# Two more places for experts' weights, and the block for tokens over capacity at the fifth quad with its loads on GpSimd

## The chip, the cores and the metric

The kernel runs on one core of one Trainium2 chip. The metric is the device time of one execution in microseconds; each kernel's time is the median of several runs. The engines are TensorE (PE in the profile; its weight loads are PEld), VectorE (DVE), ScalarE (ACT), GpSimd (POOL) and SyncE (SP), which issues nearly all transfers. Sixteen DMA engines move the data between HBM and the on-chip memory, where every tile lies over 128 partitions; a place of 8 KB per partition holds 1 MB.

## The reference

One layer over 256 tokens of width 1024, in float32: a projection to nine parts, a gated linear recurrence (hgrn2) and an attention with a bias by distance (moba, one block here) beside each other, a gated sum and an output projection, a residual with layer norm, a hierarchical mixture of experts, and a second residual with layer norm. The last part is what this change touches:

```
proj = h @ w_in[l] + b_in[l]                       # 1024 x 5632
y_a = hgrn2_mixer(...) @ w_proj_a[l]
y_b = moba_mixer(mb_q, mb_k, mb_v, rel_bias) @ w_proj_b[l]
mixed = (sigmoid(gate_a) * y_a + sigmoid(gate_b) * y_b) @ w_out[l]
x = layer_norm(DN_ALPHA * h + mixed, ...)
# hier_moe: best of 4 groups, best 2 of its 8 experts, 32 experts in all
gate, up = split(xb @ w_gate_up[e], 2)             # 1024 x (2 x 512) for each expert
y = (silu(gate) * up) @ w_down[e]                  # 512 x 1024 for each expert
x = layer_norm(DN_ALPHA * x + sum of the weighted y, ...)
```

Every expert is computed, so all weights are read once: 4 MB of `w_gate_up` and 2 MB of `w_down` for each of the 32 experts, 192 MB in all, beside some 30 MB for the projections.

## The kernel before

**The front.** The projections take their weights through four places `w_t` of 1 MB (`W_PL`), filled by `w_load` (line 108) in the order of use. Each tile is cut into four chunks of 512 columns, and ScalarE and VectorE split each chunk into a high and a low part (`split_next`, lines 280 and 281), since every product is made of three matmuls of such parts. When the fourth chunk of a tile has been split, the next `w_t` is loaded into its place. The work of hgrn2, moba and the router is written as generators that give a few instructions between the chunks (`beside`).

**The experts.** The experts go in eight quads of four (`NQ`). A quad has 24 tiles of 1 MB (`NEXP`): 16 of `w_gate_up`, each with 128 rows of two experts, and 8 of `w_down`. Each expert has room for 32 tokens (`CAP`), so a quad's tokens fill 128 columns; `gather` picks them, `by_expert` (line 1140) multiplies each expert's tokens by its weights into its own 32 partitions, `act_T` makes the activation, `y_out` and `combine` (line 1060) add the weighted result to `acc`.

**The places of the tiles `e_t`.** `E_PL` lists the places for these tiles in the order in which they come free. Four are never used for anything else, 19 to 22; the others are those of the front, once it is done with them. Tile i takes the i-th of the list (two tiles, `E_SPL` and `E_PART`, have halves elsewhere), and after the list has run out the same places go round, without the one of `acc` (`N_ACC`). `e_load(n)` issues the next n loads (line 168), at spots written out by hand: five after the third projection, two at the end of hgrn2, four at the end of moba, and so on until all places are filled, `E_NEXT` being the first tile that goes round. After that the loads stand in SP's queue in the order of the tiles, each waiting for its place; SP takes its instructions in order. Each load waits also for the load eight before it, since eight semaphores are used in turn.

```
E_NEXT = 23
E_PL = (19, 20, 21, 22, XS, H3, H4, M1, M2, M3, M4, XHI, XLO, OH, M5, 2, G1, 3, H2, 0, 1, G2)
```

**The block for tokens over capacity** (`overflow`, from line 1096). If an expert has more than 32 tokens, a loop over the experts gathers, computes and adds the further ones, with its own loads of the expert's weights in pieces of 256 KB. All engines read the highest count from memory and branch (line 1102). No expert has more than 32 tokens with these inputs, so the block is jumped over. It stands before the third quad's first matmul, behind the whole `combine` of the second; elsewhere half of a combine stands behind the second tile pair of the next quad.

Of the kernel before, what the change touches and what calls it, by code (L numbers as in the profile page):

```python
# [20 lines left out]
P = 128  # L21
# [23 lines left out]
N_ACC = 15  # L45
E_SPL = 8
E_PART = 10
E_NEXT = 23
N_WARM = (6, 1, 1, 5, 0, 14, 4)

W_PL = (0, 1, 2, 3)
XHI, XLO, XS = 4, 5, 6
H1, H2, H3, H4 = 7, 8, 9, 10
M1, M2, M3, M4, M5 = 11, 12, 13, 14, 15
OH, G1, G2 = 16, 17, 18
E_PL = (19, 20, 21, 22, XS, H3, H4, M1, M2, M3, M4, XHI, XLO, OH, M5, 2, G1, 3, H2, 0, 1, G2)


@with_exitstack
def kernel(ctx: ExitStack, tc: tile.TileContext, x, w_in, b_in, rows_in, relb, w_proj_a, w_proj_b,  # L60
                             w_out, w_router, b_router, w_gate_up, w_down, out):
    nc = tc.nc
# [8 lines left out]
    def place(i, name):  # L71

        t = big.tile([P, 2048], F32, tag=f"s{i}", name=name)
        return t[:, 0:1024], t[:, 1024:2048], t

    def part(i, name, dt=F32):
        return big.tile([P, 1024], dt, tag=f"m{i}", name=name)
# [39 lines left out]
    def e_place(i):  # L117

        i -= (i > E_SPL) + (i > E_PART)
        n = len(E_PL) - 1  # L120
        return E_PL[i] if i < n else (E_PL[:N_ACC] + E_PL[N_ACC + 1:])[(i - n) % n]

# [7 lines left out]
    def e_halves(i, halves, ns=(0, 1)):  # L130

        ts = e_tiles.setdefault(i, [None] * 2)
        for n in ns:
            nc.sync.dma_start(halves[n], e_source(i)[:, n])
            ts[n] = halves[n]

    def e_get(i):
        q, r = divmod(i, NEXP)
        if i == E_SPL:
            e_halves(i, [part(n, "e_half") for n in (1, 2)])  # L140
            return
        if i == E_PART:
            p = place(E_PL[-1], "e_t")
            e_halves(i, (part(3, "e_half"), p[0]))
            e_halves(E_NEXT, (p[1],), (0,))
            return
        t = place(e_place(i), "e_t")
        if i == E_NEXT:
            e_halves(i, (None, t[0]), (1,))
        elif q == NQ - 1 and 16 <= r < 20:  # L150

            t = t[2].rearrange("p (e c) -> p e c", e=4)
            r0 = (r - 16) * P
            nc.sync.dma_start(t, w_down[0, 4 * q:4 * q + 4, r0:r0 + P, 0:512].rearrange("e p c -> p e c"))
            e_tiles[i] = [t[:, e, :] for e in range(4)]
        elif q == NQ - 1 and r >= 20:

            nk, w = (2, 256) if r < 22 else (4, 128)
            c0, k0 = (512, 2 * (r - 20)) if r < 22 else (768 + 128 * (r - 22), 0)
            t = t[2].rearrange("p (k e c) -> p k e c", k=nk, e=4)  # L160
            for k in range(nk):
                r0 = (k0 + k) * P
                nc.sync.dma_start(t[:, k], w_down[0, 4 * q:4 * q + 4, r0:r0 + P, c0:c0 + w].rearrange(  # L163
                    "e p c -> p e c"))
            e_tiles[i] = [[t[:, k, e, :] for e in range(4)] for k in range(nk)]
        else:
            t = t[2].rearrange("p (e c) -> p e c", e=2)
            nc.sync.dma_start(t, e_source(i))  # L168
            e_tiles[i] = [t[:, e, :] for e in range(2)]
# [3 lines left out]
    def e_load(n=1):  # L173
        for _ in range(n):
            while e_next[0] in (E_SPL, E_PART):
                e_next[0] += 1
            e_get(e_next[0])
            e_next[0] += 1
# [86 lines left out]
    def places(ap, base):  # L265
        nc.gpsimd.iota(ap, pattern=[[1, ap.shape[1]]], base=base, channel_multiplier=0,
                       allow_small_or_imprecise_dtypes=True)
# [164 lines left out]
    q, scr, _ = place(H1, "h1")  # L432
# [22 lines left out]
    def rows_plus(dst, ps, row):  # L455
        for t in range(NT):
            nc.vector.tensor_tensor(dst[:, t, :], ps[:, t, :], row, op=ALU.add)
            yield
# [114 lines left out]
    queue.append(hg)  # L573
    ps = prod_N(KD, xh, xl)
    after.append(rows_plus(v, ps, bi))
    e_load(5)


    mqk = place(M1, "mqk")
# [387 lines left out]
    e_get(E_SPL)  # L967
    assert e_next[0] == E_NEXT and len(splits) == 4 * len(w_srcs)
    h_T(1, 4, 2)
# [108 lines left out]
    def late():  # L1078

        acc.extend(place(E_PL[N_ACC], "acc")[0:2])  # L1080
        for j in range(2):
# [15 lines left out]
    def overflow():  # L1097

        cmx = nc.values_load(cnt[0:1, 32:33], min_val=0, max_val=S)
        tl = work(1)  # L1100
        iov = o12.rearrange("p t a b -> p (t a b)")
        with tc.If(cmx > CAP):
            with tc.For_i(0, NE) as e:
                ce = nc.values_load(cnt[0:1, bass.ds(e, 1)], min_val=0, max_val=S)
                for g in range(2):
                    with tc.If(ce > CAP + g * P):
                        places(iov, CAP + 1 + g * P)
                        nc.vector.tensor_copy(pe[:, :, 0:1], posm[:, :, bass.ds(e, 1)])
                        nc.vector.tensor_copy(pe[:, :, 1:2], wsel[:, :, bass.ds(e, 1)])
                        xg, wT = tl["xg"], wT_of(tl["wT"])  # L1110
                        for _ in gather(lambda t: pe[:, t, 0:1], iov, tl):
                            pass
                        weigh(lambda t: pe[:, t, 1:2], P, tl)
                        gu = big2("gu")
                        for k in range(KD):
                            for j in range(2):
                                w = y_tile()[:, j * 512:(j + 1) * 512]
                                nc.sync.dma_start(w, w_gate_up[0, bass.ds(e, 1), k * P:(k + 1) * P,
                                                               j * 512:(j + 1) * 512].rearrange("e p c -> p (e c)"))
                                nc.tensor.matmul(gu[:, j, :], xg[:, k, :], w, start=(k == 0), stop=(k == KD - 1))  # L1120
                        act_T(gu)
                        py = big2("py")
                        xw = xg.rearrange("p k c -> p (k c)")
                        for k in range(4):
                            for j in range(2):
                                w = xw[:, j * 512:(j + 1) * 512]
                                nc.sync.dma_start(w, w_down[0, bass.ds(e, 1), k * P:(k + 1) * P,
                                                            j * 512:(j + 1) * 512].rearrange("e p c -> p (e c)"))
                                nc.tensor.matmul(py[:, j, :], hT_of(k), w, start=(k == 0), stop=(k == 3))
                        y_out(py)  # L1130
                        combine(wT)

            places(iota1, 1)
# [12 lines left out]
    for q in range(NQ):  # L1146
        tl = work(q)
        n0 = q * NEXP
        if q == 2:
            combine(wT_of(q - 1))  # L1150
            pending = False
            overflow()
        gu = big2("gu")
        for k in range(KD):
            if q == 0 and k == 0:
                next(feed)
                with tc.issue_after(xg_put[0].ins):
                    token_weights()
            elif q == 0 and k == 2:
                with tc.issue_after(ins):  # L1160
                    run(feed)
            for j in range(2):
                ins = by_expert(gu[:, j, :], tl["xg"][:, k, :], e_rows(n0 + 2 * k, j), k == 0, k == KD - 1,
                                pin=q == 0 and j == 0)
            if k == 1 and pending:
                combine(wT_of(q - 1))
                pending = False
            if k == 4 and q + 1 < NQ:
                with tc.issue_after(ins):
                    run(places_of(q + 1, work(q + 1)))  # L1170
                if q:
                    weigh_quad(q + 1, work(q + 1))
            if k == 5 and q == NQ - 1:
                lg2, lb2, _ = place(e_place(NQ * NEXP), "ln2")
                for r, dst in ((16, lg2), (24, lb2)):
                    for a in range(2):
                        nc.scalar.activation(dst[:, a * 512:(a + 1) * 512], spread(r + 4 * a), AF.Copy)
        act_T(gu)
        if q == 0:
            late()  # L1180
            weigh_quad(0, tl)
            weigh_quad(1, work(1))
        py = big2("py")
        if q < NQ - 1:
            for k in range(4):
                for j in range(2):
                    by_expert(py[:, j, :], hT_of(k), e_rows(n0 + 16 + 2 * k, j), k == 0, k == 3)
            y_out(py)
            pending = True
        else:  # L1190
            for k in range(4):
                by_expert(py[:, 0, :], hT_of(k), e_tile(n0 + 16 + k), k == 0, k == 3)
# [112 lines left out]
```

## Time and profile before

| | |
|---|---|
| median of 3 runs | 679.61 us (679.32 to 683.38) |
| the profiled execution | 678.75 us, span 677.1 us |
| TensorE busy | 552.7 us (82%), granted clock 0.966 of full |
| VectorE, ScalarE, GpSimd busy | 229.5, 161.8, 9.3 us |
| moved by DMA | 238.48 MB, 352 GB/s over the span |

The span goes from the first to the last instruction of one profiled execution. The page cuts it into 40 slices of 16.93 us, and gives for each the share of time that an engine was busy, the granted TensorE clock and what the DMA engines moved. Other views used below: windows (busy time of each engine, clock and GB/s in stretches of one's choice), the timeline of one engine in a stretch, the waits of one queue and what ended them, one line's or tile's instructions, and the chain of work that ended last.

### The profile page before, as it was taken

The page shows a single profiled execution, that of the slowest core. Times are in us where ns is not written, and L with a number is a line of the kernel's source. Part 1 is how long each engine was busy: PE and PEld are TensorE (multiplying, and loading weights), DVE is VectorE, ACT ScalarE, POOL GpSimd, SP SyncE. Part 2 cuts the span into 40 slices and gives each one's busy share as a digit, 9 for nine tenths or more (in the row PEclk, how much of TensorE's full clock was granted, in tenths as well). Part 3 has the DMA queues.
Part 4 walks back from the last instruction along what each step waited for, and adds up shares of the span by engine and source line. Part 5 has one row for each costly group of instructions (what it writes and reads, how often), then busy time and mean ns, then how long its engine had stood idle before and what let it go on. Part 6 is the DMA issues. An engine that isn't in the chain of part 4 may idle for free.

```text
span 677.1 us, 9744 instructions
## 1 busy us (share of the span) xinstructions
PE 552.7 (82%) x4018; PEld 313.0 (46%) x4019; DVE 229.5 (34%) x531; ACT 161.8 (24%) x321; POOL 9.3 (1%) x32
## 2 busy tenths in 40 slices
PE   8999999999998989876667767676766678678575
PEld 8989899999988453322211311131121113113123
DVE  3698768865676324120202101010201010010026
ACT  4653568955552200100100100010001001001010
POOL 1000000000000000000000000000000000000000
PEclk9999999999999969998999979998999998799989
DMA  8998366686996899989999999999999999999994
GB/s 305 368 358 262 126 249 208 229 293 204 342 383 239 325 408 409 408 315 410 410 408 410 409 409 409 410 409 409 409 410 409 410 408 410 409 409 409 404 344 132
DMA packets 78832, 238.48 MB, mean 352 GB/s; under 512 B 5182, under 2 KB 12991, under 8 KB 78783
## 3 DMA queue, kind: packets, MB, share of 16 engines
q1 hardware_dynamic: 78767, 237.80, 91.7%
q8 instruction: 33, 0.54, 0.3%
q14 instruction: 16, 0.13, 0.1%
q10 hardware_dynamic: 16, 0.01, 0.0%
HBM read 236.74 MB, written 1.06 MB: 351 GB/s over the span
## 4 chain that ended last, share of the span: by engine, by line
DMA 43%; PE 8%; SPq 2%; DVE 1%; ACT 1%; issue 0%; DVEq 0%; ACTq 0%
DMA e_t<-in_w_gate_up_dram 29%; DMA e_t<-in_w_down_dram 14%; PE gu L1140 4%; PE py L1140 2%; SPq L168 1%; PE pc L1060 1%; PE pr L1070 1%; PE pw L1204 1%; SPq L163 0%; ACT yb L1052 0%; DVE acc L1250 0%; DVE acc L1248 0%; DVE smv L807 0%; DVE yb L1043 0%; DVE yb L1044 0%
## 5 line engine op out<-in xcount | busy, mean ns | idle before, releaser
L1140 PE MATMUL gu<-e_t,xg 128*32 128x512 f32 x1012 | 168.4, 615 | 61.9 <-DMA e_t<-in_w_gate_up_dram 60.0
L1140 PEld LDWEIGHTS gu<-e_t,xg 128*32 128x32 f32 x1012 | 35.1, 110 | 176.4 <-DMA e_t<-in_w_gate_up_dram 114.4
L1140 PE MATMUL py<-e_t,hw 128*32 128x512 f32 x480 | 80.3, 680 | 28.1 <-DMA e_t<-in_w_down_dram 23.3
L281 DVE TENSOR_TENSOR w_spl<-w_t,w_spl 128x512 fp32r<-128x512 f32 x120 | 82.2, 689 | 45.3 <-ACT w_spl L280 44.7
L280 ACT ACTIVATE w_spl<-w_t 128x512 fp32r<-128x512 f32 x120 | 75.2, 631 | 72.7 <-PE psT L324 41.2
L324 PE MATMUL psT<-xT_hi,w_spl 128*128 128x256 f32 x576 | 86.7, 288 | 0.7 <-ACT w_spl L280 0.6
L324 PEld LDWEIGHTS psT<-xT_hi,w_spl 128*128 128x128 f32 x576 | 76.3, 193 | 3.6 <-ACT w_spl L280 2.0
L917 DVE TENSOR_SCALAR xg<-px,cols 128x128 f32<-128x128 f32 x32 | 12.6, 408 | 137.1 <-ACT xg L920 127.4
L1140 PEld LDWEIGHTS py<-e_t,hw 128*32 128x32 f32 x480 | 17.2, 121 | 84.5 <-DMA e_t<-in_w_down_dram 46.5
L920 ACT ACTIVATE xg<-px,cols 128x128 f32<-128x128 f32 x32 | 13.9, 455 | 176.2 <-PE px L896 170.9
L324 PE MATMUL psT<-xT_lo,w_spl 128*128 128x256 f32 x288 | 46.6, 285 | 0.0
L1053 DVE COPY yb<-py 128x512 f32<-128x512 f32 x7 | 4.8, 691 | 105.4 <-ACT yb L1052 105.4
L324 PEld LDWEIGHTS psT<-xT_lo,w_spl 128*128 128x128 f32 x288 | 40.1, 193 | 0.0
L1043 DVE TENSOR_TENSOR yb<-gu,yb 128x512 f32<-128x512 f32 x8 | 5.5, 691 | 98.8 <-ACT yb L1042 98.8
L1060 PE MATMUL pc<-yb,hw 128*128 128x512 f32 (+2 forms) x72 | 31.8, 568 | 4.9 <-ACT yb L1052 4.2
L896 PEld LDWEIGHTS px<-oh,hx 128*128 128x128 f32 x256 | 29.3, 192 | 6.7 <-issue 6.7
L1061 DVE TENSOR_TENSOR acc<-acc,pc 128x512 f32<-128x512 f32 (+2 forms) x36 | 22.5, 628 | 28.6 <-PE pc L1060 28.5
L896 PE MATMUL px<-oh,hx 128*128 128x128 f32 x256 | 31.0, 279 | 0.0
L1052 ACT ACTIVATE yb<-py 128x512 f32<-128x512 f32 x7 | 4.2, 597 | 92.1 <-PE py L1140 92.1
L1042 ACT ACTIVATE yb<-gu 128x512 f32<-128x512 f32 x8 | 4.8, 597 | 85.0 <-PE gu L1140 85.0
L1060 PEld LDWEIGHTS pc<-yb,hw 128*128 128x128 f32 x72 | 12.0, 189 | 24.7 <-ACT yb L1052 9.7
L331 PE MATMUL psN<-w_spl,mix 128*128 128x512 f32 (+1 forms) x105 | 23.3, 376 | 0.1
(235 smaller groups left out, 466.6 us busy)
## 6 DMA issues: line engine op xcount, KB each, us to landing
e_t<-in_w_gate_up_dram SPq DMA_DIRECT2D x126, 1024.0 KB, 18.6
e_t<-in_w_down_dram SPq DMA_DIRECT2D x59, 1024.0 KB, 18.5
w_t<-in_w_in_dram SPq DMA_DIRECT2D x20, 1024.0 KB, 6.2
w_t<-in_w_out_dram SPq DMA_DIRECT2D x4, 1024.0 KB, 5.9
e_t<-in_w_down_dram SPq DMA_DIRECT2D x6, 512.0 KB, 11.3
w_t<-in_w_proj_a_dram SPq DMA_DIRECT2D x2, 1024.0 KB
w_t<-in_w_proj_b_dram SPq DMA_DIRECT2D x2, 1024.0 KB, 5.0
e_t<-in_w_down_dram SPq DMA_DIRECT2D x8, 256.0 KB, 4.9
```

The costliest lines, as they stand in the source:

```text
L168: nc.sync.dma_start(t, e_source(i))
L280: ins = [nc.scalar.activation(hi, w, AF.Copy), nc.vector.tensor_tensor(lo, w, hi.bitcast(F32), op=ALU.subtract)]
L281: nc.vector.tensor_tensor(lo, w, hi.bitcast(F32), op=ALU.subtract)]
L324: nc.tensor.matmul(ps[:, c, :], a[:, c * P:(c + 1) * P], b[k], start=(k == 0 and n == 0 and c % 2 == 0), stop=(k == nk - 1 and n == 2 and ...
L331: nc.tensor.matmul(ps, a[k][:, tsl], b, start=(k == 0 and n == 0), stop=(k == nk - 1 and n == 2), skip_group_check=skip)
L896: nc.tensor.matmul(dst, hx[:, t, k * P:(k + 1) * P], oh[:, t, :], start=(k == g[0] and t == 0), stop=(k == g[-1] and t == 1), skip_group_c ...
L917: xg_put[:] = [nc.vector.tensor_scalar(xg[:, k, :], pk, g1_cols[:, k:k + 1], b1_cols[:, k:k + 1], op0=ALU.mult, op1=ALU.add)]
L920: nc.scalar.activation(xg[:, k, :], pk, AF.Identity, bias=b1_cols[:, k:k + 1], scale=g1_cols[:, k:k + 1])
L1060: nc.tensor.matmul(pc, wT[:, t * P:(t + 1) * P], y_tile()[:, sl], start=True, stop=True)
L1061: nc.vector.tensor_tensor(acc[t][:, sl], acc[t][:, sl], pc, op=ALU.add)
L1070: nc.tensor.matmul(pr[:, k * P:(k + 1) * P], ident[0:32, r + k:r + k + 1].to_broadcast([32, P]), lnr, start=True, stop=True, skip_group_ch ...
L1140: ins = nc.tensor.matmul(dst[sl], xT[:, sl], ws[e], start=first, stop=last, skip_group_check=True)
```

## The change

The places for experts' weights become 24: places 23 and 24 come from 16 KB per partition that were set aside for descriptors of transfers that GpSimd issues (`dynamic_dma_scratch_size=256` leaves 256 bytes of it). `E_NEXT` becomes 25, and the group of five early loads one of seven. The loads inside the block for tokens over capacity are issued by GpSimd and no longer by SP. The block stands before the fifth quad (q = 4).

```
-E_NEXT = 23
+E_NEXT = 25
+OVER_Q = 4
...
-E_PL = (19, 20, 21, 22, XS, H3, H4, M1, M2, M3, M4, XHI, XLO, OH, M5, 2, G1, 3, H2, 0, 1, G2)
+E_PL = (19, 20, 21, 22, 23, 24, XS, H3, H4, M1, M2, M3, M4, XHI, XLO, OH, M5, 2, G1, 3, H2, 0, 1, G2)
...
     after.append(rows_plus(v, ps, bi))
-    e_load(5)
+    e_load(7)
...
                                 w = y_tile()[:, j * 512:(j + 1) * 512]
-                                nc.sync.dma_start(w, w_gate_up[0, bass.ds(e, 1), k * P:(k + 1) * P,
+                                nc.gpsimd.dma_start(w, w_gate_up[0, bass.ds(e, 1), k * P:(k + 1) * P,
...
                                 w = xw[:, j * 512:(j + 1) * 512]
-                                nc.sync.dma_start(w, w_down[0, bass.ds(e, 1), k * P:(k + 1) * P,
+                                nc.gpsimd.dma_start(w, w_down[0, bass.ds(e, 1), k * P:(k + 1) * P,
...
-        if q == 2:
+        if q == OVER_Q:
             combine(wT_of(q - 1))
             pending = False
             overflow()
...
-    nc = _bacc.Bacc("TRN2", target_bir_lowering=False, num_devices=1)
+    nc = _bacc.Bacc("TRN2", target_bir_lowering=False, num_devices=1, dynamic_dma_scratch_size=256)
```

Lines of the changed kernel from 48 on are higher by one. Two places in the order of the built program show what moved.

The first is SP's queue in the front, from the third early load of a tile `e_t` on (`w_t` are projection weights, `wge` and `bge` the router's weights and bias, `bt` the attention's bias). Before:

```order
L168 DMA e_t<-in_w_gate_up_dram 128x2x1024
L108 DMA w_t<-in_w_in_dram 128x4x512
L168 DMA e_t<-in_w_gate_up_dram 128x2x1024
L108 DMA w_t<-in_w_in_dram 128x4x512
L686 DMA wge<-in_w_router_dram 128x8x40
L108 DMA w_t<-in_w_in_dram 128x4x512
L688 DMA bge<-in_b_router_dram 128x40
L609 DMA bt<-rel_d 128x4x256 x2
```

And now:

```order
L169 DMA e_t<-in_w_gate_up_dram 128x2x1024
L109 DMA w_t<-in_w_in_dram 128x4x512
L169 DMA e_t<-in_w_gate_up_dram 128x2x1024 x3
L109 DMA w_t<-in_w_in_dram 128x4x512 x3
L687 DMA wge<-in_w_router_dram 128x8x40
L689 DMA bge<-in_b_router_dram 128x40
L610 DMA bt<-rel_d 128x4x256
L109 DMA w_t<-in_w_in_dram 128x4x512
L610 DMA bt<-rel_d 128x4x256
```

The last early load of `e_t` has become three in a row; the router's loads and the bias table come behind one or two more loads of `w_t`.

The second is SP's path around the block for tokens over capacity: the end of the branch's part that is taken when no expert is over capacity, with the semaphores that each instruction waits for, and the first loads behind it (`DMAHW0` to `DMAHW7` are the eight semaphores by which SP's transfers report). Before:

```order
L1102 UNCONDITIONAL_BRANCH
L1102 UNCONDITIONAL_BRANCH [waits SP_sequencer_49,DMAHW0_49,DMAHW1_49,DMAHW2_49,DMAHW3_49,DMAHW4_49,DMAHW5_49,DMAHW6_49,DMAHW7_49]
L168 DMA e_t<-in_w_gate_up_dram 128x2x1024 [waits DMAHW4_49,PE_49]
L168 DMA e_t<-in_w_gate_up_dram 128x2x1024 [waits DMAHW5_49,PE_49]
L168 DMA e_t<-in_w_gate_up_dram 128x2x1024 [waits DMAHW6_49,PE_49]
```

And now:

```order
L1103 UNCONDITIONAL_BRANCH
L1103 UNCONDITIONAL_BRANCH [waits SP_sequencer_49]
L169 DMA e_t<-in_w_gate_up_dram 128x2x1024 [waits DMAHW4_49,PE_49]
L169 DMA e_t<-in_w_gate_up_dram 128x2x1024 [waits DMAHW5_49,PE_49]
L169 DMA e_t<-in_w_gate_up_dram 128x2x1024 [waits DMAHW6_49,PE_49]
```

The eight waits for SP's transfers are gone from this path. On GpSimd's path around the block there are now waits for the eight semaphores of GpSimd's own loads.

## Rows read from the trace of the kernel before

**Rows 1.** The page, 40 slices of the span: GB/s that DMA moved.

```profile
GB/s 305 368 358 262 126 249 208 229 293 204 342 383 239 325 408 409 408 315 410 410 408 410 409 409 409 410 409 409 409 410 409 410 408 410 409 409 409 404 344 132
```

**Rows 2.** Timeline of PE, 340 to 362 us; last: idle before, what ended it.

```profile
346.50 1.05 PE L1140 MATMUL py<-e_t,hw 128*32 128x512 f32 x4 [0.66 <-DMA e_t<-in_w_down_dram]
...
349.06 1.91 PE L1140 MATMUL py<-e_t,hw 128*32 128x512 f32 x12 [1.51 <-DMA e_t<-in_w_down_dram]
```

**Rows 3.** Windows in the front; last three columns: TensorE's clock, DMA share, GB/s.

```profile
core 0: us, PE busy (x) PEld busy (x) DVE busy (x) ACT busy (x) POOL busy (x), PEclk, DMA share, GB/s
...
51.00:68.00 17.00, 17.00 (x314) 16.50 (x312) 13.93 (x31) 6.31 (x10) 0.00 (x0) 1.00 0.82 261
68.00:85.00 17.00, 17.00 (x197) 14.82 (x196) 11.97 (x22) 9.41 (x18) 0.00 (x0) 1.00 0.39 127
```

**Rows 4.** Windows in the experts' stage, columns as in Rows 3.

```profile
290.00:300.00 10.00, 7.40 (x45) 2.45 (x41) 4.33 (x9) 0.60 (x1) 0.00 (x0) 1.00 0.69 249
...
294.00:296.00 2.00, 2.00 (x6) 0.95 (x5) 1.33 (x3) 0.00 (x0) 0.00 (x0) 1.00 0.30 113
...
600.00:640.00 40.00, 29.37 (x166) 9.40 (x168) 3.44 (x5) 2.66 (x5) 0.00 (x0) 1.00 1.03 409
```

**Rows 5.** Waits of SP's queue, whole run: us in total, times, longest.

```profile
SPq L168 <- PE gu L1140: 121.3, 66, 4.0
...
SPq L1102 <- SPq L1102: 17.1, 5, 5.2
```

**Rows 6.** Line 1102: count, duration in ns (min/median/max), first and last start in us.

```profile
L1102 SPq EVENT_SEMAPHORE  x9: 17/17/17, 284.3 to 296.4; - x9
...
L1102 SPq COMPARE_BRANCH  x1: 45/45/45, 279.0 to 279.0; - x1
...
L1102 PEldq COMPARE_BRANCH  x1: 3772/3772/3772, 294.9 to 294.9; - x1
```

**Rows 7.** Timeline of SP's queue, 40 to 72 us: start, us, line.

```profile
44.06 0.46 SPq L168 DMA_DIRECT2D e_t<-in_w_gate_up_dram  x1
50.09 0.37 SPq L108 DMA_DIRECT2D w_t<-in_w_in_dram  x1
...
69.56 0.37 SPq L108 DMA_DIRECT2D w_t<-in_w_in_dram  x1
```

**Rows 8.** Timeline of SP's queue, 216 to 226 us.

```profile
222.00 0.33 SPq L134 DMA_DIRECT2D e_t<-in_w_down_dram  x1
```

**Rows 9.** The page's DMA issues: count, KB each, median us to landing.

```profile
e_t<-in_w_gate_up_dram SPq DMA_DIRECT2D x126, 1024.0 KB, 18.6
...
w_t<-in_w_in_dram SPq DMA_DIRECT2D x20, 1024.0 KB, 6.2
```

**Rows 10.** Tiles bt and wge, first readers: ns each, first and last start in us.

```profile
L630 DVE TENSOR_TENSOR pm<-psc,bt x4: 409/409/414, 102.1 to 103.7; 128x256 f32<-128x256 f32 x4
...
L695 DVE TENSOR_TENSOR wb<-wge,cols x1: 482/482/482, 89.9 to 89.9; 128x320 f32<-128x320 f32 x1
```

**Rows 11.** Timeline of PE, 290 to 300 us, around the block.

```profile
293.56 3.70 PE L1060 MATMUL pc<-yb,hw 128*128 128x512 f32 x8 [0.74 <-ACT yb L1052]
299.12 1.45 PE L1140 MATMUL gu<-e_t,xg 128*32 128x512 f32 x9 [1.86 <-PEq L1102]
```

**Rows 12.** Chain of work that ended last, 640 to 677 us: start, us, what.

```profile
647.76 1.15 PE py L1140 x8
648.91 3.48 PE pw L1204 x4
652.38 2.76 PE py L1140 x24
...
655.81 2.00 PE pc L1060 x4
...
665.01 0.47 PE py_c L1140 x8
...
665.83 0.50 PE pc L1060 x2
```

## The prediction

> **What bounds the kernel now.** I read the profile in this order: the page's rows over 40 slices, the windows view, the waits of SP's queue, the timeline.
>
> The page's row of GB/s [rows 1] splits the run in two. Up to about 220 us the transfers run at 126 to 383 GB/s; from the fifteenth slice up to the last three, where the work runs out, they stand at 408 to 410 GB/s, with one exception: the eighteenth slice, 315. In this second part TensorE stands still until a load lands: its matmuls on an experts' tile start at 346.50 and at 349.06 us, each released by a transfer of `e_t`, 2.56 us apart [rows 2]. A tile is 1024 KB, and 1.0486 MB at 409 GB/s is also 2.56 us. So the stage of the experts lasts as long as its bytes. There are two ways to shorten it: have more tiles loaded before it begins, or close holes in the stream.
>
> The first part is bound elsewhere: TensorE is busy 17.00 of 17.00 us from 51 to 85 us while the transfers take only 261 and 127 GB/s there [rows 3]. Bytes moved in that stretch cost nothing, as long as no projection weight comes late for them.
>
> The one hole lies at the block for tokens over capacity. The windows view gives 249 GB/s from 290 to 300 us and 113 from 294 to 296, against 409 later [rows 4]. SP's queue tells why: it waited 17.1 us in five pieces on line 1102, its branch around the block [rows 5]. The branch itself stands at 279.0; nine semaphore waits follow at 284.3 to 296.4 [rows 6]. The order of SP's rows names them: its own and the eight by which its transfers report. Nothing was queued while SP waited for all that was in flight, so the 16 engines ran dry. The block itself did no work in this run: the page lists no load from its lines.
>
> **The change part by part.**
>
> *Two more places.* The order shows where they are used: two more loads of `e_t` in SP's queue behind the one issued at 44.06 us [rows 7]. Every later load of a tile then carries an index higher by two, and 2 x 2.56 = **5.13 us** of transfer leave the second part. The gain would be lost if the stream still stood at the start of that part for lack of a place. It does stand: SP takes up its loads again at 222.00 [rows 8], when TensorE frees the first place. But that moment is TensorE's, and the stock there is two tiles larger; nothing in the wait itself changes.
>
> What the two loads cost: they put 5.13 us of transfer ahead of the next projection weights. Between 51 and 85 us the engines could have moved (1 - 261/409) x 17 + (1 - 127/409) x 17 = 17.9 us more [rows 3], so the backlog is gone by 85 us. The load of `w_t` issued at 50.09 lands some 6.2 us later [rows 9], at 56.3. Such a load is issued when a tile has been used up, and there are four tiles; so this one is read when three more are done, which the load issued at 69.56 marks [rows 7]. The slack is 13.3 us against a delay of at most 5.13: cost nothing. The cover is that slack; without it each us would be paid in full, since TensorE has no pause there. The bias table `bt` and the router's weights `wge` go behind one or two more loads of `w_t`, to some 63 to 70 us; they are first read at 102.1 and 89.9 us [rows 10]. Nothing for them either.
>
> *Loads of the block from GpSimd.* They never run here. What counts is the path around the block: SP now waits for its own sequencer's semaphore alone, as the order shows, and GpSimd waits for semaphores of loads that have not been issued. So SP's queue goes on. The hole is (409 - 249) x 10 / 409 = **3.91 us** [rows 4]; the eighteenth slice gives the same, (409 - 315) x 16.93 / 409 = 3.89 [rows 1]. The bounds: nothing, if something else drains the queue at the new spot, and 3.91, if nothing does. I take 3.91, since the rows of the order no longer hold the waits that made it.
>
> SP still jumps over the block. From its branch at 279.0 to its first semaphore at 284.3 pass 5.3 us in which it issues nothing [rows 6]. I cost a pause of that length at nothing in the stream: a load takes 18.6 us from issue to landing [rows 9], so some seven are under way and the engines have work for three times the pause. The Trainium skill (Runtime: NRT & Kernel Launch, Instruction fetch mechanics) says that a taken branch out of the window of fetched instructions must wait for a fetch. Those 5.3 us, and TensorE's own 3772 ns on the same branch, agree with it; by this rule the jump gets shorter on SP and longer on GpSimd, whose loads it must now pass.
>
> *The block at the fifth quad.* TensorE pays there what it pays now before the third: all eight matmuls of the combine in one run, 3.70 us, where the other quads have half of them behind the first tiles, and a pause of 1.86 us at the branch [rows 11]. At the fifth quad TensorE waits for loads anyhow and, with the pause over, finds two or three tiles landed; 23 places against some seven loads under way leave room for many more. Cost nothing. GpSimd's weighing for the next quad comes four tiles on, off the path. At the program's end SP waits for eight more semaphores in four instructions; nine such waits took 17 ns each once fulfilled [rows 6], so under 0.1 us.
>
> *The sum.* 5.13 + 3.91 = 9.04 us. The profiled execution took 678.75 us: 669.7. The median of the runs, 679.61, is 0.86 above it; the same sum takes it to **670.6 us**, 1.3% less. For the rate of the stream, the Trainium skill (DMA: Bandwidth & Descriptors, Specifications) states an HBM limit of about 358 GB/s per core. An estimate by that page's figure makes the two tiles 5.86 us and the sum 9.8; the rows show 409, and the sum stays at 9.04.
>
> **The rivals.**
>
> *Only one of the two terms comes.* If the queue is drained at the fifth quad too, by a wait that the order doesn't show me, 5.13 remain: 674.5. Against it: SP's waits on eight semaphores are gone from its rows. If the two loads merely push later ones, so that the stock at 222 us is not larger, 3.91 remain: 675.7. Against it: the idle 17.9 us of the front, and the stream at 383 GB/s and below even in the best slice before that. Chance 6% each.
>
> *TensorE paces the loads.* SP's waits are mostly put down to TensorE: 121.3 us in 66 pieces on matmuls of `gu` [rows 5]. If a place freed by TensorE is really what each issue waits for, then TensorE's stop at the fifth quad lands on the path. Its price is the pause of 1.86 and half the combine's run, 3.70 / 2 = 1.85: 3.71 less gain, 674.3. Against it: no slice after the eighteenth falls below 408 GB/s before the last three, whatever TensorE does at the turns of the quads. Such a wait ends without the stream ever running dry. The Trainium skill's rule on the taken branch, cited above, stands beside this rival: by it the branch has its pause at any spot. Chance 5%.
>
> *Slower: the tail at the lower clock.* After the last full tile the chain runs over TensorE: 1.15, 3.48, 2.76 and 2.00 us from 647.76 on, then 0.47 and 0.50 after the last landing [rows 12]; four matmuls that take 3.48 us show that some of it is slow already. If TensorE, which waits for more of the shortened stage, gets only 1.2 instead of 2.4 GHz through all of this, its 10.36 us double at most. The change decides for slower where this adds more than 9.04 us; the full price gives 670.6 + 10.4 = 681.0. Against it: the tail stands behind the same sequence of loads as now, only earlier, and the loads cover part of it. Chance 3%.
>
> *That the change doesn't do what it says* is excluded by the order for the two loads and for SP's waits; that leaves a general 2%.
>
> **How the numbers follow.** Both terms whole: 78%, with its own range 669.0 to 672.5 (0.3 us of doubt in the hole, the rest the spread of the runs). The range takes in the places alone and TensorE's pacing, 674.5 and 674.3: 668.5 to 675.0 leaves out the hole alone, the slower tail and the unknown. A measurement of this kernel can tell about 1% from no change, here 6.8 us: below 672.8 it counts as faster. Only the first case lies there, and a little of it may miss: 0.76. The two single terms and the pacing make no change, 0.20; slower 0.04.
>
> **What would show each step.** In the profile after: three loads of `e_t` in a row near 44 us and higher GB/s from 51 to 85, with TensorE still at 17.00 of 17.00; no slice under 408 GB/s between some 240 and 640 us; SP's waits on its branch line gone or a single one of up to 5 us; the stage's landings 5.1 us earlier before the third quad and 9.0 after. Wrong would be a new dip at the fifth quad, a pause of TensorE for `w_t` between 60 and 90 us, or a stretch from the last landing to the end that is longer than now.

## The result, and the profile after

| | before | the change |
|---|---|---|
| median | 680.01 us (679.32 to 683.38, 4 runs) | 670.67 us (670.20 to 670.90, 4 runs) |
| the profiled execution | 678.75 us, span 677.1 us | 670.60 us, span 669.0 us |

The ratio is 0.9852, with a 95% interval of 0.9819 to 0.9885, which lies wholly under 1. The medians lie 9.3 us apart, the two profiled executions 8.15 us. The forecast was 670.6 us. In two later series the change was run again beside the kernel before: 671.28 us, ratio 0.9879 (0.9857 to 0.9900), and 671.38 us, ratio 0.9859 (0.9837 to 0.9881).

The page of the change, GB/s over 40 slices of 16.73 us, answers to [rows 1]:

```profile
GB/s 306 380 373 310 193 252 201 237 286 207 334 389 263 252 409 408 409 411 408 408 410 409 409 409 409 408 409 410 408 410 409 410 409 409 409 410 408 403 340 125
```

The slice of 315 is gone: from the fifteenth slice to the thirty-seventh none is under 408. The fourth and fifth, which were 262 and 126, are now 310 and 193: that is where the two additional tiles went.

SP's queue in the front (start, us, line), beside [rows 7]:

```profile
42.48 0.37 SPq L109 DMA_DIRECT2D w_t<-in_w_in_dram  x1
42.90 2.81 SPq L169 DMA_DIRECT2D e_t<-in_w_gate_up_dram  x3
48.96 13.20 SPq L109 DMA_DIRECT2D w_t<-in_w_in_dram  x3
```

and the windows of the front and of the experts' stage, beside [rows 3, 4] (us, PE, PEld, DVE, ACT and POOL busy, PEclk, DMA share, GB/s):

```profile
51.00:68.00 17.00, 17.00 (x314) 16.48 (x313) 13.25 (x28) 6.31 (x10) 0.00 (x0) 1.00 0.86 300
68.00:85.00 17.00, 17.00 (x136) 14.73 (x135) 11.62 (x21) 9.15 (x18) 0.00 (x0) 1.00 0.61 189
...
290.00:300.00 10.00, 9.26 (x60) 2.64 (x56) 3.45 (x5) 0.60 (x1) 0.00 (x0) 1.00 1.02 409
...
410.00:450.00 40.00, 29.62 (x168) 10.10 (x170) 6.55 (x15) 2.20 (x6) 0.80 (x2) 0.87 1.03 408
```

TensorE is busy 17.00 of 17.00 us in both windows of the front, as before, while (300 - 261) x 17 + (189 - 127) x 17 = 1717 KB more are moved, the most of two tiles. At 290 us, where the block was, the stream runs at 409 instead of 249. Around the block's new place, 410 to 450 us, it runs at 408.

Line 1103 is the branch around the block (count, ns, first and last start), beside [rows 6]:

```profile
L1103 SPq COMPARE_BRANCH  x1: 50/50/50, 399.2 to 399.2; - x1
L1103 SPq EVENT_SEMAPHORE  x1: 17/17/17, 399.3 to 399.3; - x1
...
L1103 POOLq COMPARE_BRANCH  x1: 45/45/45, 379.7 to 379.7; - x1
L1103 POOLq EVENT_SEMAPHORE  x6: 17/30/43, 385.0 to 385.5; - x6
...
L1103 PEldq COMPARE_BRANCH  x1: 6152/6152/6152, 411.6 to 411.6; - x1
```

SP passes it in 0.1 us with a single semaphore, where it had nine in 17.4 us. The 5.3 us between the branch and the first semaphore, which were SP's, are now GpSimd's (379.7 to 385.0). SP's waits on this line, the second row of [rows 5], no longer occur.

TensorE's timeline around the new place (start, us, and in brackets the idle time before and what ended it), beside [rows 11]:

```profile
410.26 3.70 PE L1061 MATMUL pc<-yb,hw 128*128 128x512 f32 x8 [0.70 <-ACT yb L1053]
418.20 7.38 PE L1141 MATMUL gu<-e_t,xg 128*32 128x512 f32 x44 [4.24 <-PEq L1103]
```

TensorE stands still for 4.24 us at the branch, longer than the 1.86 before, and then runs 44 matmuls without a pause: it works off the tiles that landed meanwhile.

Where the 8.15 us of the two profiles come from is read from the landings of the same load in both traces; all loads that SP issues are counted from the start, those of the projections too. The 98th load, ahead of the block's old place, landed at 293.69 us and now at 289.07, 4.6 us earlier; the 101st, behind it, at 305.26 and now at 296.75, 8.5 earlier. From there the lead varies between 7.3 and 8.8 and ends at 8.15. The tail is not longer than before. In the chain that ended last, beside [rows 12]:

```profile
640.10 1.93 PE py L1141 x8
642.03 3.43 PE pw L1205 x4
645.46 2.76 PE py L1141 x24
...
656.87 0.47 PE py_c L1141 x8
...
657.69 0.50 PE pc L1061 x2
```

From the last tile's matmuls to the span's end it is 669.0 - 656.87 = 12.1 us, before 677.1 - 665.01 = 12.1. From the first of the rows to the end it is 28.9 us, before 677.1 - 647.76 = 29.3.

### The profile page after: what moved, and what is told of

Its sections match the earlier page's. It is cut to its first block, busy times and chain, and to the rows that moved or that the text cites. A ratio compares the mean times of both kernels' runs of the same rounds, so it can differ in the third digit from the quotient of the medians.

```text
span 669.0 us, 9743 instructions
## 1 busy us (share of the span) xinstructions
PE 555.9 (83%) x4018; PEld 311.9 (47%) x4019; DVE 229.3 (34%) x531; ACT 162.2 (24%) x321; POOL 9.2 (1%) x32
## 4 chain that ended last, share of the span: by engine, by line
DMA 46%; PE 45%; DVE 3%; SPq 3%; ACT 2%; issue 1%; DVEq 0%; ACTq 0%
DMA e_t<-in_w_gate_up_dram 30%; PE psT L325 17%; DMA e_t<-in_w_down_dram 14%; PE gu L1141 8%; PE psN L332 7%; PE py L1141 4%; SPq L169 2%; PE px L897 2%; PE pr L1071 1%; PE pc L1061 1%; DMA xs<-in_x_dram 1%; PE pl L487 1%; PE pg L836 1%; PE pw L1205 1%; PE pom L672 0%
## 5 line engine op out<-in xcount | busy, mean ns | idle before, releaser
L1141 PE MATMUL py<-e_t,hw 128*32 128x512 f32 x480 | 87.3, 744 | 25.1 <-DMA e_t<-in_w_down_dram 20.3
```

The costliest lines, as they stand in the source:

```text
L1141: ins = nc.tensor.matmul(dst[sl], xT[:, sl], ws[e], start=first, stop=last, skip_group_check=True)
```

## The experiments

The theory has two terms: two places take 5.13 us of transfer out of the second part, and the block's loads on GpSimd close a hole of 3.91 us in the stream; the block's new place costs and brings nothing. The rivals: only one of the terms comes, or TensorE's stop at the block paces the loads. Each series was run beside the kernel before on one chip; ratios are to that kernel.

| kernel | median us (range) | ratio (95%) |
|---|---|---|
| first series: before | 680.32 (677.83 to 682.48) | |
| e1_places | 675.18 (674.98 to 676.46) | 0.9926 (0.9901 to 0.9951) |
| e2_block | 675.83 (674.36 to 676.96) | 0.9929 (0.9903 to 0.9954) |
| e3_q2 | 672.18 (670.68 to 673.89) | 0.9879 (0.9852 to 0.9907) |
| e4_sp | 675.77 (671.88 to 677.63) | 0.9930 (0.9908 to 0.9951) |
| second series: before | 678.98 (677.79 to 681.63) | |
| again (the change) | 671.28 (670.21 to 672.20) | 0.9879 (0.9857 to 0.9900) |
| e5_noblock | 672.07 (671.81 to 674.40) | 0.9892 (0.9871 to 0.9913) |
| e6_one | 673.41 (671.58 to 674.22) | 0.9908 (0.9888 to 0.9929) |
| e8_twice | 671.11 (669.23 to 672.93) | 0.9872 (0.9849 to 0.9895) |
| third series: before | 680.70 (678.75 to 683.77) | |
| again2 (the change) | 671.38 (670.68 to 672.21) | 0.9859 (0.9837 to 0.9881) |
| e9_warm | 670.47 (668.59 to 673.39) | 0.9857 (0.9832 to 0.9881) |
| e10_cold | 671.47 (670.64 to 672.16) | 0.9861 (0.9838 to 0.9883) |

### The places alone (e1_places)

The change, with the block where it was and its loads on SP:

```diff
-OVER_Q = 4
+OVER_Q = 2
...
-                                nc.gpsimd.dma_start(w, w_gate_up[0, bass.ds(e, 1), ...
+                                nc.sync.dma_start(w, w_gate_up[0, bass.ds(e, 1), ...
```

(the same for `w_down`).

> The two places alone: the block stands before the third quad again and its loads are SP's. The forecast's theory: two tiles less in the bound stage, 5.1 us under the kernel before (ratio 0.9925), SP again waits 15 to 18 us on its branch line, and the hole of 3.9 us is still there near 290 us. Rival (the stream restarts badly after the front, as the profile of the change hints with 180 GB/s from 224 to 226 us): only 3.5 us or less. Rival (TensorE paces the loads): no statement of its own here, 5.1 as well.

It took 5.14 us less than before, against the 5.13 expected; the interval of its ratio reaches from 3.3 to 6.7 us, so the nearness is chance. Its page keeps the hole, in the eighteenth slice:

```profile
GB/s 309 386 376 301 185 247 229 206 313 188 359 386 223 270 408 410 407 301 409 409 408 409 409 410 408 409 410 409 409 410 409 410 408 409 409 410 409 405 345 131
```

SP's waits on the branch line, and two microseconds of its windows:

```profile
SPq L1103 <- SPq L1103: 16.8, 5, 5.2
```

```profile
292.00:294.00 2.00, 1.26 (x13) 0.34 (x6) 0.23 (x1) 0.60 (x1) 0.00 (x0) 1.00 0.01 2
```

SP waits 16.8 us there, nearly as long as in [rows 5], and at 2 GB/s the engines are all but dry. The places pay by themselves, and they leave the hole alone.

### The block alone (e2_block)

The kernel before, with its 22 places:

```diff
+OVER_Q = 4
...
-                                nc.sync.dma_start(w, w_gate_up[0, bass.ds(e, 1), ...
+                                nc.gpsimd.dma_start(w, w_gate_up[0, bass.ds(e, 1), ...
...
-        if q == 2:
+        if q == OVER_Q:
```

(`w_down` likewise; the descriptors' space stays as it was).

> The block's part alone: 22 places as before, the block before the fifth quad, its loads from GpSimd. The forecast's theory: the hole goes, 3.9 us under the kernel before (ratio 0.9943), no slice under 405 GB/s between 240 and 630 us. Rival (TensorE paces the loads): at most 0.2 us, since TensorE's stop of 4 to 6 us at the fifth quad takes back what the hole gave.

It took 4.5 us less, where 3.9 were expected; the ratio expected lies in the interval, and the rival's 0.2 us (ratio 0.9997) outside it. The two windows of the block's old and new place:

```profile
290.00:300.00 10.00, 9.26 (x58) 2.67 (x51) 2.06 (x3) 0.60 (x1) 0.00 (x0) 0.94 1.03 410
410.00:420.00 10.00, 7.15 (x26) 1.85 (x23) 1.72 (x3) 0.60 (x1) 0.00 (x0) 0.83 1.03 410
```

No hole in either. Both terms exist without the other, so "only one of the two comes" has fallen.

### Which half of the block's edit (e3_q2, e4_sp)

The change with the block at its old place, its loads on GpSimd:

```diff
-OVER_Q = 4
+OVER_Q = 2
```

> The change with the block back before the third quad, its loads still from GpSimd. The forecast's theory: the spot is worth nothing, only SP's eight waits count: 9.0 to 9.3 us under the kernel before (ratio 0.986), as the change itself. Rival (the spot matters, since the stream needs the stock of the early quads): 2 to 4 us less of the gain, with a dip in GB/s near 290 us.

And the change with the block at the fifth quad, its loads back on SP:

```diff
-                                nc.gpsimd.dma_start(w, w_gate_up[0, bass.ds(e, 1), ...
+                                nc.sync.dma_start(w, w_gate_up[0, bass.ds(e, 1), ...
```

> The change with the block's loads back on SP, the block still before the fifth quad. The forecast's theory: SP drains its queue there, the hole of some 3.9 us stands near 410 us in place of 290 us, and 5.1 us under the kernel before are left (ratio 0.9925). Rival (the spot alone, not the queue, made the hole go): 9.0 us, no hole.

With the loads on GpSimd the time at the old place is 672.18 us, 8.1 under the kernel before, where 9.0 to 9.3 were expected; its ratio, 0.9879, is the same as the change's in the second series, and the expected 0.986 lies in its interval. It differs from e1_places in the queue of the block's loads alone: that queue is worth 675.18 - 672.18 = 3.0 us, and the ranges of the two don't meet. At the new place with the loads on SP the time is 675.77, 4.6 under the kernel before, where 5.1 were expected. Its ratio of 0.9930 lies outside the intervals of all three series of the change, from which it differs in the queue alone. The page of e4_sp shows the hole at the block's new place, in the twenty-fifth slice, and a window shows its bottom:

```profile
GB/s 306 382 377 304 191 248 216 225 295 208 336 393 243 290 409 408 408 409 409 407 410 409 409 408 318 414 409 409 409 409 409 409 409 410 409 409 409 405 351 127
```

```profile
412.00:414.00 2.00, 0.54 (x2) 0.00 (x0) 1.10 (x2) 0.00 (x0) 0.00 (x0) 1.00 0.20 82
```

```profile
SPq L1103 <- SPq L1103: 16.1, 5, 5.3
```

By that slice the hole is (409 - 318) x 16.78 / 409 = 3.7 us.

The landings show the hole without the spread of the medians. Between the 98th and the 101st load the lead over the trace of the kernel before grows by 3.85 to 3.90 us in every trace in which SP does not wait at the old place: three of the change and those of eight variants, e4_sp among them. In e1_places, where SP waits there, it changes by -0.1. In e4_sp it then falls at the new place from 9.34 to 5.96 us, between the 146th and the 148th load. The profiled execution of e4_sp took only 672.83 us, about as long as that of e3_q2 (672.20), although it has the hole: its experts' loads started again at 220.76 us, those of e3_q2 at 222.53. Two single executions can't be compared for a term of this size.

So the hole goes with the queue that carries the block's loads, wherever the block stands; moving the block brings nothing and costs nothing that these runs can show.

### Is the block still paid for (e5_noblock, e8_twice)

Without the block, so that tokens over capacity, which these inputs don't have, would be left out:

```diff
-            overflow()
```

> The change without the block for tokens over capacity and without its branch (tokens over capacity would be dropped; there are none). The forecast's theory: what is left of the block costs nothing, so the same time as the change within 0.7 us. Rival (TensorE paces the loads): TensorE's pause at the branch (4.24 us in the profile of the change) is on the path, 4 us or more under the change.

And with a second copy of it before the sixth quad:

```diff
-        if q == OVER_Q:
+        if q in (OVER_Q, OVER_Q + 1):
```

> The change with a second copy of the block before the sixth quad, jumped over as well. The forecast's theory: TensorE's second pause of some 4 us is hidden behind the loads: the same time as the change within 0.7 us, no slice under 405 GB/s in the stage. Rival (TensorE paces the loads): 4 us or more over the change.

Without it the kernel took 672.07 us, with two copies 671.11, with one 671.28. That is 0.8 us more and 0.2 us less than the change; 0.8 is a little over the 0.7 expected, and both ratios agree with the change's within their intervals. TensorE pays its stop twice in e8_twice (line 1103), and the stream does not notice either (two windows, the first and the second copy):

```profile
L1103 PEldq COMPARE_BRANCH  x2: 6112/6117/6122, 412.6 to 476.9; - x2
```

```profile
412.00:424.00 12.00, 7.79 (x39) 2.68 (x39) 3.25 (x6) 0.00 (x0) 0.00 (x0) 0.86 1.03 407
476.00:490.00 14.00, 9.87 (x47) 3.43 (x49) 4.12 (x9) 0.00 (x0) 0.00 (x0) 0.76 1.03 407
```

If TensorE paced the loads, one stop more or less would show with the pause at the branch, 4.24 us in the trace of the change. It does not, in either direction, and 4.24 us, 0.0062 of the time, is more than the half widths of two of these intervals together (0.0021 to 0.0023 each): that rival has fallen.

### One place (e6_one)

```diff
-E_NEXT = 25
+E_NEXT = 24
...
-E_PL = (19, 20, 21, 22, 23, 24, XS, ...
+E_PL = (19, 20, 21, 22, 23, XS, ...
...
-    e_load(7)
+    e_load(6)
```

> The change with one place more than before in place of two. The forecast's theory: each place is worth 2.56 us, so 6.5 us under the kernel before (ratio 0.9905), between the change and the block's part alone. Rival (the stock is not what counts, the front's order of loads is): as the change or as no place, 9.0 or 3.9.

It took 673.41 us, 2.1 us more than the change beside it, where one tile's transfer is 2.56. Its ratio, 0.9908, is near the 0.9905 expected, and the rivals' (9.0 us, 0.9867, and 3.9 us, 0.9943) lie outside its interval, which does overlap that of the change. Two windows of its front lie between those of before and of the change:

```profile
51.00:68.00 17.00, 17.00 (x314) 16.48 (x314) 13.27 (x28) 6.31 (x10) 0.00 (x0) 1.00 0.82 270
68.00:85.00 17.00, 17.00 (x134) 14.62 (x133) 11.13 (x21) 9.60 (x18) 0.00 (x0) 1.00 0.48 157
```

In these two windows one place brings (270 - 261 + 157 - 127) x 17 = 663 KB more than before, two places 1717 KB. From 34 to 51 us, where the additional loads are issued, the stream ran at 353 GB/s before, 379 with one place and 375 with two, which adds 442 and 374 KB. Together that is 1105 and 2091 KB, close to the 1049 of one tile and the 2097 of two: each place adds its megabyte in the front.

### The change again (again, again2)

> The change itself once more, beside the other kernels of this call. 9.0 to 9.3 us under the kernel before (ratio 0.986). If the weak restart of the stream near 225 us in the first profile belongs to the kernel, it stands here again (below 300 GB/s from 224 to 226 us); if it is chance, the stream is at 370 GB/s or more there, as in the kernel before.

> The change once more, beside the two kernels that vary the front's end. Ratio to the kernel before 0.9865, give or take 0.002. The run of 26 matmuls of the gather at 215 to 217 us takes either 3.15 us (first place freed near 220.9) or 4.77 us (near 222.3).

The second came out as expected, 0.9859. The first was 7.7 us under the kernel before, where 9.0 to 9.3 were expected; the expected ratio 0.986 lies in its interval. Its question on the weak restart is answered by the windows from 224 to 226 us of the kernel before, of the first trace of the change and of again:

```profile
224.00:226.00 2.00, 2.00 (x21) 0.91 (x24) 1.38 (x4) 0.46 (x1) 0.76 (x2) 1.00 0.96 369
...
224.00:226.00 2.00, 2.00 (x24) 0.57 (x20) 0.41 (x1) 0.37 (x1) 0.13 (x1) 1.00 0.46 180
...
224.00:226.00 2.00, 2.00 (x20) 1.10 (x22) 1.40 (x6) 0.46 (x1) 0.80 (x2) 1.00 0.77 256
```

At 256 GB/s, and 274 in again2, it stands again, so by the rule set there it belongs to the kernel. But that is not settled: e9_warm, which loads in the same order, reached 354 there, and e2_block, with the places of before, 264. Why is not shown.

The two profiled executions took 1.6 and 0.8 us more than that of the first result. Again2's trace shows one reason, where the stream is started for the second part (timeline of PE and of SP's queue):

```profile
215.37 0.38 PE L856 MATMUL pp<-sel,oh 128*128 128x32 f32 x2 [1.65 <-DVE sel L853]
...
215.84 4.75 PE L897 MATMUL px<-oh,hx 128*128 128x128 f32 x26
```

```profile
222.47 0.33 SPq L135 DMA_DIRECT2D e_t<-in_w_gate_up_dram  x1
```

```profile
216.00:220.00 4.00, 4.00 (x24) 4.00 (x24) 0.69 (x3) 0.46 (x1) 0.00 (x0) 0.60 0.16 62
```

In the first trace of the change this gather of 26 matmuls took 3.15 us at a granted clock of 1.00, and the first place came free at 220.87. Here it took 4.75 us; the granted clock from 216 to 220 us (third column from the end) is 0.60, so most of it ran at 1.2 instead of 2.4 GHz, after a pause of 1.65 us in which TensorE waited for VectorE. The first trace has the same pause, 1.66 us, so its length alone does not decide.

### The pause before the gather (e9_warm, e10_cold)

Before that pause TensorE runs eight matmuls whose result is not used. One kernel has ten more of them, the other has none:

```diff
-N_WARM = (6, 1, 1, 5, 0, 14, 4)
+N_WARM = (6, 1, 1, 5, 0, 14, 9)     # e9_warm
+N_WARM = (6, 1, 1, 5, 0, 14, 0)     # e10_cold
```

> The change with ten more idle matmul steps on TensorE (1.4 us by the eight that take 1.14) in its pause of 1.66 us before the second half of the gather's routing. If that pause is what lets the granted clock fall to its lower level in some executions, the gather's 26 matmuls take 3.15 us here, the first place is freed near 220.8, and the median is 0 to 1.6 us under the change beside it, most likely 0.8. If the spread of the restart comes from the start-up alone, the gather may take 4.77 us here too, and the median is that of the change within 0.5 us.

> The change without the eight idle matmul steps ahead of that pause, so that it lasts some 2.8 us. If the pause lowers the clock, the gather's 26 matmuls take 4.77 us, the first place is freed 1.6 us later than where they take 3.15, and the median is 0 to 1.6 us over the change beside it. If TensorE's clock at this spot doesn't set the stream's restart, the median is that of the change within 0.5 us.

The traces went as the theory said. The rows of e9_warm, and its windows over the gather and over 18 us from SP's first load:

```profile
215.38 0.38 PE L856 MATMUL pp<-sel,oh 128*128 128x32 f32 x2 [0.54 <-DVE sel L853]
...
215.81 3.15 PE L897 MATMUL px<-oh,hx 128*128 128x128 f32 x26
```

```profile
216.00:220.00 4.00, 4.00 (x38) 3.19 (x41) 1.15 (x5) 0.92 (x2) 0.00 (x0) 1.00 0.20 79
...
220.84:238.84 18.00, 16.90 (x150) 7.57 (x142) 5.03 (x22) 3.53 (x15) 1.60 (x4) 1.00 0.93 367
```

and of e10_cold:

```profile
214.64 0.60 PE L856 MATMUL pp<-sel,oh 128*128 128x32 f32 x2 [2.63 <-DVE sel L853]
...
215.48 5.69 PE L897 MATMUL px<-oh,hx 128*128 128x128 f32 x26
```

```profile
216.00:220.00 4.00, 4.00 (x21) 4.00 (x20) 0.43 (x2) 0.46 (x1) 0.00 (x0) 0.50 0.05 18
```

The gather took 3.15 us behind a pause of 0.54, and 5.69 behind one of 2.63; the first place came free at 220.84 and at 223.06 us. The medians can't tell: e10_cold took 671.47 us against 671.38 of the change beside it, though it starts the stream later, and e9_warm's 670.47 is 0.9 us less, as expected, but its runs spread from 668.59 to 673.39. In these traces, one execution each, the clock fell with the longer pause and held with the shorter one; that this is worth a time is not shown. No version beat the change by more than the runs can tell.

## Why the prediction was right

**What bounds the kernel.** The second part lasts as long as its bytes. After the change TensorE's matmuls are released by landings of `e_t` as before, at the same distance, only earlier:

```profile
337.69 1.05 PE L1141 MATMUL py<-e_t,hw 128*32 128x512 f32 x4 [0.65 <-DMA e_t<-in_w_down_dram]
340.26 1.91 PE L1141 MATMUL py<-e_t,hw 128*32 128x512 f32 x12 [1.51 <-DMA e_t<-in_w_down_dram]
```

These are the matmuls of [rows 2], which stood at 346.50 and 349.06: 8.8 us earlier, again 2.57 us apart.

**Two places, 5.13 us.** Shown by e1_places (5.14) and, for one of them, by e6_one (2.1 of 2.56); e3_q2 against e2_block, which differ in the places and in the spot, gives 3.7. The size is shown only as well as these medians can tell, to some 1.7 us. In the profiled pair only 4.6 us had been gained when the block's old place was reached, although SP's first load of the second part could go at 220.87 instead of 222.00. The stream started less well there, as the first 18 us from that load show, before and after:

```profile
222.00:240.00 18.00, 16.89 (x150) 7.57 (x142) 5.03 (x22) 3.51 (x14) 1.59 (x4) 1.00 0.96 374
...
220.87:238.87 18.00, 16.90 (x150) 7.57 (x142) 5.03 (x22) 3.52 (x14) 1.60 (x4) 1.00 0.86 337
```

(374 - 337) x 18 / 409 = 1.6 us is what this start cost, and 5.13 + 1.13 - 1.63 = 4.63 is the lead that was read. The forecast has neither of these two terms: it took the start of the stream as unchanged. Counted in the same way, again had 341 GB/s, again2 350, e9_warm 367 and e10_cold 373. SP issues its first eight loads at the same distances in the trace before and in that of the change; why the transfers were slower stays open.

**The cost of the two loads, nothing.** TensorE has no pause in the front's windows. The load of `w_t` behind the two, issued at 48.96, took 10.9 us to landing; in the trace before, the one issued at 50.09 took 5.3. That is a delay of 5.6 us, a little over the 5.13 forecast as the most. It landed at 59.8; its tile is read from about 68.4 on, when the third load of `w_t` behind it was issued.

**The hole, 3.91 us.** Shown by e2_block (4.5), by e1_places against e3_q2 (3.0, the queue alone), and by the landings of the profiled pair: 8.5 - 4.6 = 3.9. Its cause is as predicted. SP's drain of its own eight semaphores goes with the block's loads, since e4_sp brings the waits and the hole back at another place.

**SP's jump.** The 5.3 us that were costed at nothing did not just stay hidden, they went away: SP takes 0.1 us, and GpSimd has the 5.3. The Trainium skill (Runtime: NRT & Kernel Launch, Instruction fetch mechanics), by which a branch out of the fetched window waits for a fetch, had led to this: the trace agrees, since the engine whose queue holds the block's loads is the one with the long jump. In e1_places and e4_sp, with the loads on SP, SP has 5.2 and 5.3 us again and GpSimd 0.4. No run shows the fetch itself.

**The block at the fifth quad, nothing.** That it costs nothing was right, and a size was off: TensorE's pause is 4.24 us and not 1.86. The tiles that lie ready cover it, as the run of 44 matmuls shows, and e8_twice shows it for two such stops.

**The tail at the lower clock.** It did not come: 12.1 us from the last landing's matmuls to the end, as before, and 28.9 from the tail's first rows, before 29.3.

**The sum.** 9.04 us were forecast. The medians gave 9.3, 7.7 and 9.3 in three series, and the profiled pair 8.15. That the median, 670.67, meets the forecast of 670.6 to 0.1 us is luck: it was counted from 679.61, where the series of the result has 680.01, and the interval is some 2.2 us wide on either side. What is shown is the two terms, each to a microsecond or two. The stream's rate held at 408 to 411 GB/s from the fifteenth slice to the thirty-seventh. The Trainium skill (DMA: Bandwidth & Descriptors, Specifications) gives about 358 GB/s per core; an estimate by that figure made the sum 9.8. The trace does not agree, and the measured rate decides.

## What to carry to other kernels

Where a stage lasts as long as its transfers, every megabyte that an earlier stage can move while its own bound is elsewhere comes off the end at the stage's rate, and this can be priced before it is built. How well the stream starts is a term of its own: here it moved by more than a microsecond from one execution to the next, so a term of a few microseconds is judged by medians or landing by landing, not by one pair of spans. Look for single dips in an otherwise flat row of GB/s, and read which queue's waits stand there: a branch around transfers that never run can still drain the queue that would issue them, and giving those transfers to a queue with nothing in flight closes the dip. A stop of the compute engine in such a stage, here of some 4 us, did not show in the time while landed tiles lay ready behind it.

## What the runs showed of the hardware

TensorE's branch around the same block took 3772 ns before [rows 6], 6152 with the change, 6372 in e1_places at the old place and with the loads on SP, and 4092 in e4_sp at the new one. In all traces with the loads on GpSimd, at either place, it took 6032 to 6172. So neither the place nor the queue alone sets it; what does was not found. Leaving the stop out, or paying it twice, did not show in the time (e5_noblock, e8_twice).

A pause of TensorE of 1.65 us was followed by a granted clock of 1.00 from 216 to 220 us in one execution of the change and of 0.60 in another; with 0.54 us of pause it was at 1.00, and with 2.63 us at 0.50, where the gather took 5.69 us instead of 3.15. The executions of one kernel differ by 1.6 us in this one run of matmuls.
